# The middle tap and the bias of a width-3 depthwise convolution, moved from VectorE to ScalarE, in a two-layer diffusion backbone

## The chip, the cores and the metric

The kernel runs on one core of one Trainium2 chip. The metric is the device time of one execution in microseconds (us): the time before is the median of three runs, and a profile of one further execution shows where that time lies. The engines are named as the profile names them: PE is TensorE's matmul and PEld its weight load, DVE is VectorE, ACT is ScalarE, POOL is GpSimd, SP is SyncE, which here issues the loads.

## The reference, cut to what matters

Two layers (DEPTH 2) act on 128 context and 512 latent tokens of width 1024. Each layer has four attention branches, a merge, and a gated MLP with a centred depthwise convolution of width 3 between the up-projection and the activation:

```python
def _conv_ffn(h, lp):
    u = h @ lp['w_up']                      # D_FF = 2816, so 5632 channels
    up = jnp.pad(u, ((0, 0), (half, half), (0, 0)))
    acc = lp['conv_b'] + up[:, 0:T] * lp['conv_w'][0]
    for j in range(1, CONV_W):
        acc = acc + up[:, j:j + T] * lp['conv_w'][j]
    a, g = jnp.split(acc, 2, axis=-1)
    return (jax.nn.silu(g) * a) @ lp['w_down']
```

Context and latent tokens are convolved apart. Each residual branch is scaled by a gate that comes out of a linear map of SiLU(cond), the adaLN modulation: six sections of 1024 values a layer, two for each of shift, scale and gate. Section 5 is the MLP's gate.

## The kernel before

Activations lie with channels on the 128 partitions and the 640 tokens along the free axis, and each product is made in two halves of 320 columns. Every fp32 operand is split into a high part (written `wh`, `hH`: ScalarE) and a low part (`wl`, `hL`: VectorE, original minus high part), and a product is three matmuls: high by high, high by low, low by high (`passes`, L952).

The order of the instructions on each engine is made by a planner that runs when the program is built (L189 to L480). Pieces of work are generators. The dense ones (projections) are taken from one queue in a fixed order; the others (norms, attention, convolution, activation, modulation) run beside them by priority. The planner keeps an estimated clock for each engine: `act` (L292) adds 93 + 0.8333 ns for each element to ScalarE's clock, and 93 more for each scale or bias that is a tile; `clk("V", ...)` adds to VectorE's. Whatever may start by these clocks is written down next. The engines then run their instructions in the written order and wait at semaphores.

In the MLP, `up_gen` (L1373) makes one unit of 128 channels `u` in two halves of 24 matmuls each, and ScalarE moves the halves from PSUM to `u` (L386 to L390). `conv` (L1331) then makes `y` of 128x641 in three VectorE instructions: L1337 is the middle tap and the bias, and the two `stt` calls add the outer taps in place. `chain` (L1345) takes a pair of units, an `a` and a `g`: ScalarE's tanh, VectorE's products, a ScalarE and a VectorE split. `down_gen` (L1398) multiplies the result by `w_down`, group by group. Weights come in by SP into three buffers `raw`; ScalarE makes `wh`, VectorE `wl`.

The modulation for the later sections is worked off in the background by `ada_bg` (L752), in half sections: eight loads, each with two VectorE multiply-adds into two accumulators (L790 to L797), then for both accumulators a high part on ScalarE and a low part on VectorE (L804, L808), four matmuls by `selR` (L812), the split of the resulting row into `rowR`, high part on ScalarE, low part on VectorE (L815, L816), and after the second half the four matmuls `sel<-rowR` (L823). This generator does not go on while ScalarE's or VectorE's planned clock is more than 1000 ns ahead of PE's. `down_gen` begins only when section 5 is ready:

```python
        yield lambda: ("act", l, fs[0]) in done and ("ada", l, 3) in done
```

so the last dense work that may be written in front of the first down-projection of a layer is the seventh pair of up-projection units, and `sel<-rowR` of section 5 stands in front of the first down-projection in PE's order.

Of the kernel before, what the change touches and what calls it, by code (L numbers as in the profile page):

```python
# [13 lines left out]
AF = mybir.ActivationFunctionType  # L14
OP = mybir.AluOpType
# [173 lines left out]
def emit(nc, tc, t):  # L189
# [18 lines left out]
    class S:  # L208
        pe = 0.0
        cur = 0.0  # L210
        c = NC_SLOT
# [17 lines left out]
    def clk(e, cost, port=False):  # L229
        s = max(C[e], S.cur)  # L230
        if port:
            s = max(s, C["X"])
            C["X"] = s + cost - (130 if e == "G" else 0)
        C[e] = s + cost
        S.cur = s + cost + S.t[0]
# [15 lines left out]
    def Q(dt=F):  # L251
        return G(dt, False)

    def rel(*ts):
        for x in ts:
            k, _ = KIND.pop(id(x))
            if k == "c":
                S.c += 1
            else:
                S.g += 1  # L260
# [25 lines left out]
    def fsize(ap):  # L286
        n = 1
        for s in ap.shape[1:]:
            n *= s
        return n  # L290

    def act(out, in_, func, **kw):  # L292
        c = (52 if psum(in_) else 93) + 0.8333 * fsize(out)
        if TAB.get(func, tab[0]) != tab[0]:
            tab[0] = TAB[func]
            c += 1283
        for k in ("scale", "bias"):
            if not isinstance(kw.get(k, 0.0), (int, float)):
                c += 93
        if "accum_out" in kw:  # L300
            c += 93
        clk("A", c)
        nc.scalar.activation(out, in_, func, **kw)  # L303

    def psum(ap):
        return ap.tensor.space == bass.MemoryType.PSUM
# [38 lines left out]
    def stt(out, a, s, b, op0, op1):  # L345
        clk("V", (67 if isinstance(s, float) else 129) + 1.042 * fsize(out), two(a, b))
        nc.vector.scalar_tensor_tensor(out, a, s, b, op0=op0, op1=op1)  # L347
# [59 lines left out]
    def spawn(gen, prio, keep=(0, 0), lim=None):  # L407
        th = Th(gen, prio, keep, lim)
        th.ready = S.cur
        i = 0  # L410
        while i < len(ths) and ths[i].prio <= prio:
            i += 1
        ths.insert(i, th)
# [917 lines left out]
    def conv(l, f, s):  # L1331
        yield 1
        u = UB.pop((f, s))
        y = Q()
        c = VECS[l][:, V_CV:V_CV + 176].rearrange("p (c j) -> p c j", j=4)[:, s * NF + f]
        clk("V", 520)
        nc.vector.tensor_scalar(y[:, :641], u[:, 1:642], c[:, 1:2], c[:, 3:4], op0=OP.mult, op1=OP.add)  # L1337
        stt(y[:, :641], u[:, 0:641], c[:, 0:1], y[:, :641], OP.mult, OP.add)
        stt(y[:, :641], u[:, 2:643], c[:, 2:3], y[:, :641], OP.mult, OP.add)
        rel(u)  # L1340
        YB[f, s] = y
        if s == 1:
            spawn(chain(l, f), 2)

    def chain(l, f):  # L1345
        yield lambda: (f, 0) in YB
        yield 3
        a, g = YB.pop((f, 0)), YB.pop((f, 1))
        th = Q()
        H, L = Q(R), Q(R)  # L1350
        act(th[:, :641], g[:, :641], AF.Tanh, scale=0.5)
        yield
        stt(g[:, :641], th[:, :641], 1.0, g[:, :641], OP.add, OP.mult)
        tt(th[:, 0:128], a[:, 0:128], g[:, 0:128], OP.mult)
        tt(th[:, 128:640], a[:, 129:641], g[:, 129:641], OP.mult)
        rel(a, g)
        yield
        split_h(H[:, :NT], th[:, :NT], 0.5)
        yield
        split_l(H[:, :NT], L[:, :NT], th[:, :NT], 0.5)  # L1360
        rel(th)
        ACTS[f] = (H, L)
        yield
        done.add(("act", l, f))
# [8 lines left out]
    def up_gen(l, f, s, part):  # L1373
        yield N(c=1 if part != 1 else 0, cond=has("h4", l, 1, part if part < 2 else 1))
        gk = gate(l, 1, part if part < 2 else 1)
        u = u_tile(f, s) if part != 1 else UB[f, s]
        V = yield from W3("a", s, f, 8)
        for hh, (a, b) in enumerate(HC):
            if part < 2 and hh != part:
                continue  # L1380
            yield N(d=1)
            pd = PD()
            yield from half_mm(pd[:, :HN], V, 8, hH, hL, hh, gk=gk)
            S.cur = S.pe + S.t[1]
            if hh == 0:
                act(u[:, 1:129], pd[:, 0:128], AF.Copy)
                S.cur = S.pe + S.t[1]
                act(u[:, 130:322], pd[:, 128:320], AF.Copy)
            else:
                act(u[:, 322:642], pd[:, :HN], AF.Copy)  # L1390
            free("d")
        wrel()
        if part:
            spawn(conv(l, f, s), 2)
# [841 lines left out]
```

## Time and profile before

| | |
|---|---|
| median of three runs | 2325.96 us (2325.31 to 2327.69) |
| the profiled execution | 2329.46 us, of which the span from first to last instruction is 2327.7 us |
| mean granted TensorE clock | 0.991 of full speed |
| busy share of the span | PE 98%, DVE 77%, ACT 48%, POOL 13% |
| chain that ended last | PE 76%, DVE 13%, ACT 4%, DMA 3%, issue 3% |
| the MLP of layer 0, of layer 1 | about 730 to 1190 us, about 1870 to 2328 us |

Matmuls are pipelined, so PE's busy time is not its peak; the gaps between its instructions are what can be read. A wait is put down to the engine that released it last.

### The profile page before, as it was taken

To read this page: it belongs to the slowest core of one execution; us is meant where nothing else is said; L and a number is where in the kernel's file an instruction comes from. 1 tells how busy PE (TensorE), PEld (TensorE's weight loads), DVE (VectorE), ACT (ScalarE), POOL (GpSimd) and SP (SyncE) were. 2 spreads that over 40 slices of the span, in tenths; PEclk is the share of its full clock that TensorE was granted. 3 is DMA by queue.
4 is the path that set the end of the run, shared out by engine and by line. 5 is a ranking of instruction groups with operands and counts; after the bars stand their busy time and mean duration, and the time that the engine had idled before them with its cause. 6 is when DMAs were issued, how large, how long until landed. Compare 5 with 4: busy or idle time off the path is not lost.

```text
span 2327.7 us, 40730 instructions
## 1 busy us (share of the span) xinstructions
PE 2273.9 (98%) x15480; PEld 2195.2 (94%) x15480; DVE 1800.1 (77%) x3399; ACT 1125.4 (48%) x2419; POOL 300.1 (13%) x563
## 2 busy tenths in 40 slices
PE   8899999999999999999999999999999999999999
PEld 3899999999999999999999989999999999999999
DVE  5678878878779888766677788887879997565566
ACT  4467767664344323233355676666534542323232
POOL 0112112312021000000022121132111200000000
PEclk9999999999999999999999999999999999999999
DMA  7632323335554342322264332233456432221313
GB/s 255 235 122 73 112 82 110 100 127 175 196 186 137 105 155 93 125 78 68 87 202 155 121 114 82 87 111 109 145 179 225 172 114 85 85 74 59 98 51 132
DMA packets 114018, 292.18 MB, mean 126 GB/s; under 512 B 15840, under 2 KB 24736, under 8 KB 113824
## 3 DMA queue, kind: packets, MB, share of 16 engines
q1 hardware_dynamic: 105664, 258.43, 33.8%
q0 software_dynamic: 8160, 31.15, 3.6%
q8 instruction: 122, 2.00, 0.4%
q14 instruction: 72, 0.59, 0.1%
HBM read 257.59 MB, written 31.95 MB: 124 GB/s over the span
## 4 chain that ended last, share of the span: by engine, by line
PE 76%; DVE 13%; ACT 4%; DMA 3%; issue 3%; SPq 0%; POOL 0%; DVEq 0%; ACTq 0%; POOLq 0%
PE d L368 63%; PE ps L368 10%; DVE c L347 3%; PE po L368 2%; DVE wl L332 2%; DMA c<-w_ada 2%; DVE c L332 1%; ACT wh L303 1%; DVE p L347 1%; DVE hL L347 1%; DVE g L332 1%; ACT ps L303 1%; DMA g<-sp 1%; ACT c L325 1%; ACT c L303 0%
## 5 line engine op out<-in xcount | busy, mean ns | idle before, releaser
L368 PE MATMUL d<-hH,wh 128*128 128x320 f32 x2432 | 760.4, 313 | 0.4 <-ACT hH L303 0.4
L368 PE MATMUL d<-hL,wh 128*128 128x320 f32 x2432 | 754.7, 310 | 3.4 <-DVE hL L347 3.4
L368 PE MATMUL d<-hH,wl 128*128 128x320 f32 x2432 | 753.9, 310 | 0.8 <-DVE wl L332 0.8
L368 PEld LDWEIGHTS d<-hL,wh 128*128 128x128 f32 x2432 | 460.1, 189 | 7.6 <-DVE hL L347 5.0
L368 PEld LDWEIGHTS d<-hH,wh 128*128 128x128 f32 x2432 | 459.9, 189 | 4.1 <-ACT hH L303 0.7
L368 PEld LDWEIGHTS d<-hH,wl 128*128 128x128 f32 x2432 | 459.5, 189 | 1.1 <-DVE wl L332 1.1
L303 ACT ACTIVATE wh<-raw 128x1024 fp32r<-128x1024 f32 (+4 forms) x344 | 333.7, 971 | 206.2 <-PE d L368 178.4
L368 PE MATMUL d<-c,wh 128*128 128x320 f32 x1776 | 411.5, 311 | 2.8 <-DVE c L347 1.1
L332 DVE TENSOR_TENSOR wl<-raw,wh 128x1024 fp32r<-128x1024 f32 (+4 forms) x344 | 383.4, 1115 | 35.1 <-ACT wh L303 33.0
L303 ACT ACTIVATE c<-d 128x320 f32<-128x320 f32 (+2 forms) x376 | 130.7, 372 | 389.6 <-PE d L368 384.2
L368 PEld LDWEIGHTS d<-c,wh 128*128 128x128 f32 x1776 | 300.6, 189 | 7.8 <-DVE c L347 2.2
L368 PE MATMUL d<-c,wl 128*128 128x320 f32 x960 | 297.1, 309 | 0.0
L368 PE MATMUL d<-wh,hH 128*128 128x256 f32 (+1 forms) x720 | 208.7, 290 | 3.9 <-ACT wh L303 2.4
L347 DVE SCALAR_TENSOR_TENSOR c<-c,cs,c 128x512 f32<-128x512 f32 x266 | 198.0, 791 | 15.9 <-DMA c<-w_ada 15.9
L368 PE MATMUL d<-wh,hL 128*128 128x256 f32 (+1 forms) x720 | 205.1, 285 | 3.4 <-DVE hL L347 3.4
L368 PE MATMUL d<-wl,hH 128*128 128x256 f32 (+1 forms) x720 | 205.3, 285 | 1.0 <-DVE wl L332 1.0
L303 ACT ACTIVATE c<-c 128x641 f32<-128x641 f32 (+8 forms) x197 | 127.8, 665 | 161.1 <-DVE c L347 78.4
L368 PEld LDWEIGHTS d<-c,wl 128*128 128x128 f32 x960 | 180.9, 188 | 0.0
L347 DVE SCALAR_TENSOR_TENSOR c<-c,vec,c 128x641 f32<-128x641 f32 x174 | 154.6, 888 | 12.7 <-DVE c L347 0.5
L368 PE MATMUL d<-g,wh 128*128 128x320 f32 x656 | 158.9, 309 | 0.0
L1337 DVE TENSOR_SCALAR c<-c,vec 128x641 f32<-128x641 f32 x87 | 53.5, 614 | 124.7 <-ACT c L303 121.5
L368 PEld LDWEIGHTS d<-wh,hH 128*128 128x128 f32 x720 | 138.1, 192 | 5.1 <-ACT wh L303 2.6
(196 smaller groups left out, 3449.2 us busy)
## 6 DMA issues: line engine op xcount, KB each, us to landing
raw<-wst SPq DMA_DIRECT2D x264, 512.0 KB
c<-w_ada SPq DMA_DIRECT2D x184, 256.0 KB
mgd<-c POOLq DMA_DIRECT2D x46, 320.0 KB, 3.2
raw<-wst SPq DMA_DIRECT2D x32, 320.0 KB
c<-mgd SPq DMA_DIRECT2D x30, 320.0 KB
raw<-wst SPq DMA_DIRECT2D x32, 256.0 KB
c<-rpb SPq DMA_DIRECT2D x24, 320.0 KB
c<-xin SPq DMA_DIRECT2D x16, 320.0 KB
```

Of the source, the lines that this page charges most:

```text
L303: nc.scalar.activation(out, in_, func, **kw)
L325: nc.scalar.copy(out, in_)
L332: nc.vector.tensor_tensor(out, a, b, op=op)
L347: nc.vector.scalar_tensor_tensor(out, a, s, b, op0=op0, op1=op1)
L368: nc.tensor.matmul(out, lhsT, rhs, start=start, stop=stop, skip_group_check=True)
L1337: nc.vector.tensor_scalar(y[:, :641], u[:, 1:642], c[:, 1:2], c[:, 3:4], op0=OP.mult, op1=OP.add)
```

## The change

L1336 and L1337, a planned cost of 520 ns and one VectorE instruction, become one ScalarE activation with the function Identity, whose scale and bias are columns of the tile `vec`. The two VectorE instructions that follow read and write the same `y` as before. The convolution is made for 44 units in each of the two layers.

```diff
         c = VECS[l][:, V_CV:V_CV + 176].rearrange("p (c j) -> p c j", j=4)[:, s * NF + f]
-        clk("V", 520)
-        nc.vector.tensor_scalar(y[:, :641], u[:, 1:642], c[:, 1:2], c[:, 3:4], op0=OP.mult, op1=OP.add)
+        act(y[:, :641], u[:, 1:642], AF.Identity, scale=c[:, 1:2], bias=c[:, 3:4])
         stt(y[:, :641], u[:, 0:641], c[:, 0:1], y[:, :641], OP.mult, OP.add)
         stt(y[:, :641], u[:, 2:643], c[:, 2:3], y[:, :641], OP.mult, OP.add)
```

By `act` the planner now charges ScalarE 93 + 0.8333 x 641 + 2 x 93 = 813 ns, and since its clocks move, it writes some of the other work down in another place. On PE the dense matmuls keep their order. In both layers' MLPs the background matmuls of the modulation stand elsewhere among them; the attention parts of both layers are in the old order on every engine.

The first place is layer 0, section 5 of the modulation in front of the first down-projection. On PE before, `ps<-...selR` are the four matmuls of the second half section, `d1842` is the last half of an up-projection, `d1851` the first down-projection (its operands are `c` tiles):

```order
L368 MATMUL d1842_9830<-hH2_102,wl1819_9656 128x320
L368 MATMUL ps1843_9840<-c1829_9750,selR_89 2x512
L368 MATMUL ps1843_9840<-c1830_9751,selR_89 2x512
L368 MATMUL ps1843_9840<-c1831_9752,selR_89 2x512
L368 MATMUL ps1843_9840<-c1832_9753,selR_89 2x512
L368 MATMUL d1842_9830<-hH3_103,wh1815_9632 128x320
L368 MATMUL d1842_9830<-hL3_111,wh1815_9632 128x320
L368 MATMUL d1842_9830<-hH3_103,wl1819_9656 128x320
```

Fifteen matmuls of `d1842`, of which the last three rows are the first, follow the four, and then `sel<-rowR` and `d1851`. The same place on PE in the changed kernel, where the last half of the up-projection is `d1838` and the first down-projection `d1857`:

```order
L368 MATMUL d1838_9820<-hL7_115,wh1815_9623 128x320
L368 MATMUL d1838_9820<-hH7_107,wl1819_9646 128x320
L368 MATMUL ps1850_9873<-c1840_9850,selR_89 2x512
L368 MATMUL ps1850_9873<-c1841_9851,selR_89 2x512
L368 MATMUL ps1850_9873<-g1842_9852,selR_89 2x512
L368 MATMUL ps1850_9873<-g1843_9853,selR_89 2x512
L368 MATMUL ps1851_9882<-sel4_91,rowR_94 128x4 x4
L368 MATMUL d1857_9895<-c1739_9052,wh1822_9698 128x320
```

The four `selR` matmuls have moved behind the last up-projection, and nothing stands between them and `sel<-rowR`. VectorE at this place in the changed kernel, where `g1844` is the convolution of the unit that `d1838` completes, `c1841` and `g1843` are the low parts that `selR` reads, and `rowR` is the low part that `sel<-rowR` reads:

```order
L347 SCALAR_TENSOR_TENSOR g1794_9443<-g1796_9445,cs_124,g1794_9443 128x512
L347 SCALAR_TENSOR_TENSOR g1844_9856<-c1833_9779,vec0_128,g1844_9856 128x641 x2
L332 TENSOR_TENSOR wl1845_9860<-raw1820_9648,wh1839_9848 128x640
L332 TENSOR_TENSOR c1841_9851<-c1793_9442,c1840_9850 128x512
L332 TENSOR_TENSOR g1843_9853<-g1794_9443,g1842_9852 128x512
L347 SCALAR_TENSOR_TENSOR g1844_9856<-c1847_9866,g1844_9856 128x641
L332 TENSOR_TENSOR c1847_9866<-c1835_9791,g1844_9856 128x128
L332 TENSOR_TENSOR c1847_9866<-c1835_9791,g1844_9856 128x512
L332 TENSOR_TENSOR rowR_94<-ps1850_9873,rowR_94 2x512
```

The low parts for `selR` now stand behind the outer taps of the last unit; before they stood two units earlier, and the last unit's convolution came behind `rowR`. ScalarE at this place in the changed kernel; `c1833<-d1838` empties the last half of the up-projection, and `g1844<-c1833,vec0` is the new instruction:

```order
L303 ACTIVATE c1833_9779<-d1838_9820 128x320
L303 ACTIVATE wh1839_9848<-raw1820_9648 128x640
L303 ACTIVATE c1840_9850<-c1793_9442 128x512
L303 ACTIVATE g1842_9852<-g1794_9443 128x512
L303 ACTIVATE g1844_9856<-c1833_9779,vec0_128 128x641
L303 ACTIVATE c1847_9866<-g1844_9856 128x641
L303 ACTIVATE rowR_94<-ps1850_9873 2x512
```

The new instruction stands behind a weight split and the two high parts, all of them behind the emptying of `d1838`.

The second place is the same one in layer 1. VectorE before; `c4147` and `c4149` are the low parts for `selR`, `c4151` is the last unit's convolution:

```order
L347 SCALAR_TENSOR_TENSOR g4138_23156<-c4136_23154,g4137_23155 128x640
L332 TENSOR_TENSOR c4147_23241<-c4100_22862,c4146_23240 128x512
L332 TENSOR_TENSOR c4149_23243<-c4101_22863,c4148_23242 128x512
L1337 TENSOR_SCALAR c4151_23266<-c4140_23189,vec1_135 128x641
L347 SCALAR_TENSOR_TENSOR c4151_23266<-c4140_23189,vec1_135,c4151_23266 128x641 x2
L332 TENSOR_TENSOR wl4152_23270<-raw4127_23060,wh4150_23264 128x640
L332 TENSOR_TENSOR rowR_94<-ps4154_23274,rowR_94 2x512
```

And VectorE in layer 1 in the changed kernel, where `c4148` and `c4150` are those low parts:

```order
L347 SCALAR_TENSOR_TENSOR c4101_22869<-c4103_22871,cs_124,c4101_22869 128x512
L347 SCALAR_TENSOR_TENSOR c4151_23264<-c4140_23187,vec1_135,c4151_23264 128x641 x2
L332 TENSOR_TENSOR wl4152_23268<-raw4127_23056,wh4146_23256 128x640
L332 TENSOR_TENSOR c4148_23259<-c4100_22868,c4147_23258 128x512
L332 TENSOR_TENSOR c4150_23261<-c4101_22869,c4149_23260 128x512
L347 SCALAR_TENSOR_TENSOR c4151_23264<-c4154_23274,c4151_23264 128x641
L332 TENSOR_TENSOR c4154_23274<-c4142_23199,c4151_23264 128x128
L332 TENSOR_TENSOR c4154_23274<-c4142_23199,c4151_23264 128x512
L332 TENSOR_TENSOR rowR_94<-ps4157_23281,rowR_94 2x512
```

The low parts have moved from in front of the last unit's convolution to behind it, and `rowR` behind three more rows. PE in layer 1 has `selR`, `sel<-rowR` and the first down-projection directly behind the last up-projection in both kernels, and ScalarE stands there as in layer 0.

## Rows read from the trace of the kernel before

**Rows 1.** The page: busy us of each engine, share of the span, instructions.

```profile
PE 2273.9 (98%) x15480; PEld 2195.2 (94%) x15480; DVE 1800.1 (77%) x3399; ACT 1125.4 (48%) x2419; POOL 300.1 (13%) x563
```

**Rows 2.** Stretches: us, busy PE, PEld, DVE, ACT, POOL (instructions), granted clock, DMA.

```profile
730.00:1190.00 460.00, 459.38 (x3118) 455.64 (x3118) 355.76 (x549) 159.72 (x295) 21.79 (x128) 1.00 0.34 107
1870.00:2328.00 458.00, 450.08 (x3051) 448.39 (x3050) 302.27 (x450) 139.80 (x253) 6.39 (x117) 1.00 0.26 86
...
820.00:840.00 20.00, 20.00 (x138) 20.00 (x138) 19.90 (x37) 4.45 (x6) 0.00 (x0) 1.00 0.54 181
```

**Rows 3.** PE's waits in the two MLPs: us in total, times, longest.

```profile
PE d L368 <- ACT hH L303: 0.4, 1, 0.4
...
PE ps L368 <- DVE rowR L332: 3.7, 1, 3.7
```

**Rows 4.** PE in order of time, layer 1, around the first down-projection.

```profile
1950.73 1.08 PE L368 MATMUL ps<-c,selR 128*2 128x512 f32 x4
1955.50 0.61 PE L368 MATMUL ps<-sel,rowR 98*128 98x4 f32 x4 [3.68 <-DVE rowR L332]
1955.97 0.79 PE L368 MATMUL d<-c,wh 128*128 128x320 f32 x2
...
1959.49 0.31 PE L368 MATMUL d<-g,wh 128*128 128x320 f32 x1
```

**Rows 5.** The granted clock behind that wait: busy us of PE, PEclk.

```profile
1957.00:1959.00 2.00, 2.00 (x10) 0.50 0.06 20
```

**Rows 6.** ACT in order of time, layer 1, the same stretch.

```profile
1947.86 1.15 ACT L303 ACTIVATE c<-c 128x512 fp32r<-128x512 f32 x2
1950.93 0.44 ACT L303 ACTIVATE c<-d 128x320 f32<-128x320 f32 x1 [1.92 <-PE d L368]
1951.27 0.73 ACT L303 ACTIVATE wh<-raw 128x640 fp32r<-128x640 f32 x1
1952.02 0.58 ACT L303 ACTIVATE rowR<-ps 2x512 fp32r<-2x512 f32 x1
```

**Rows 7.** DVE in order of time, layer 1, the same stretch.

```profile
1949.58 1.29 DVE L332 TENSOR_TENSOR c<-c,c 128x512 fp32r<-128x512 f32 x2
1951.46 0.62 DVE L1337 TENSOR_SCALAR c<-c,vec 128x641 f32<-128x641 f32 x1 [0.60 <-issue]
1952.12 1.88 DVE L347 SCALAR_TENSOR_TENSOR c<-c,vec,c 128x641 f32<-128x641 f32 x2
1953.91 0.82 DVE L332 TENSOR_TENSOR wl<-raw,wh 128x640 fp32r<-128x640 f32 x1
1954.76 0.68 DVE L332 TENSOR_TENSOR rowR<-ps,rowR 2x512 fp32r<-2x512 f32 x1
1955.48 0.83 DVE L347 SCALAR_TENSOR_TENSOR c<-c,c 128x641 f32<-128x641 f32 x1
1956.34 0.89 DVE L332 TENSOR_TENSOR c<-c,c 128x128 f32<-128x128 f32 x2
```

**Rows 8.** PE in order of time, layer 0, around the first down-projection.

```profile
812.28 1.09 PE L368 MATMUL ps<-c,selR 128*2 128x512 f32 x4
813.21 0.31 PE L368 MATMUL d<-hH,wh 128*128 128x320 f32 x1
...
815.42 0.51 PE L368 MATMUL ps<-sel,rowR 98*128 98x4 f32 x4
815.78 0.54 PE L368 MATMUL d<-c,wh 128*128 128x320 f32 x2
```

**Rows 9.** Groups by line and shape: count, busy us, mean ns, idle before and releaser.

```profile
L1337 DVE TENSOR_SCALAR c<-c,vec 128x641 f32<-128x641 f32 x87 | 53.5, 614 | 124.7 <-ACT c L303 121.5 <-issue 2.9
L303 ACT ACTIVATE c<-c 128x641 f32<-128x641 f32 x42 | 31.2, 743 | 67.6 <-DVE c L347 65.5 <-issue 2.1
L303 ACT ACTIVATE hH<-c,ad,gs 128x320 fp32r<-128x320 f32 x8 | 4.9, 643 | 0.0
L303 ACT ACTIVATE hH<-c,ad,gs 128x128 fp32r<-128x128 f32 x8 | 3.9, 482 | 10.6 <-DVE gs L631 10.6
```

## The prediction, made before the changed kernel ran

> **What bounds the kernel now.** I read the page's first part, then the busy time by stretches, then PE's waits in the two MLPs, since the convolution runs nowhere else, and last PE, ACT and DVE in order of time where PE waits. The page has PE busy for 98% of the span and DVE for 77% [rows 1]. PE is pipelined, so that figure alone proves little; what counts is that in layer 0's MLP PE is busy 459.38 of 460 us and that its longest wait there is 0.4 us [rows 2, 3]. DVE is busy 355.76 us of the same 460 and ACT 159.72 [rows 2]; in places DVE is full, as with 19.90 of 20 us between 820 and 840, and PE still runs through [rows 2]. So DVE is loaded but hidden: the MLP lasts as long as its matmuls do. Layer 1's MLP is the same but for one wait of 3.7 us, PE for DVE's `rowR` [rows 3]. There PE ends the four `selR` matmuls, has nothing but `sel<-rowR` written next, and stands until 1955.50 [rows 4]. Between 1957 and 1959 the clock is granted at 0.50, that is 1.2 of 2.4 GHz [rows 5]. The matmuls' usual pitch is 0.147 us (15 of them between 813.21 and 815.42 in [rows 8]); from 1955.97 to 1959.49 thirteen take 3.52 us where they would take 1.91, so the wait costs another 1.6 us in clock [rows 4].
>
> **What the change removes.** 88 DVE instructions of 614 ns, 54 us of DVE [rows 9]. PE waited for DVE for almost nothing, so as busy time this is worth nothing; it could gain only what is in the 3.7 + 1.6 us of layer 1.
>
> **What it adds.** 88 activations on ACT. None of this shape with two tile operands is in the trace. The lower bound is 743 ns, the tanh of 128x641 without them [rows 9]. With both, 128x128 takes 482 ns and 128x320 643 ns, 0.84 ns for each further column, which gives 912 ns at 641 [rows 9]. I take 0.91 us, since that row has the same operands: 80 us on ACT. ACT has 300 of 460 us free in layer 0's MLP [rows 2], so this too is hidden as busy time. Two rules of the notes frame it. The Trainium skill, ScalarE: Activation LUTs, section Rules for kernel authors, says to give multiplications and additions to VectorE and not to ScalarE; by that rule each moved instruction is 0.3 us dearer here, 26 us in all if ScalarE set the pace, which the rows on its free time speak against. The Trainium skill, Perfetto Trace Analysis, section Optimizing Scalar/DVE Operations, says that moving work to ScalarE may pay where VectorE is saturated; by that rule the late `rowR` of layer 1 would come earlier, and the trace agrees with its premise only between such points as 820 to 840.
>
> **What it moves.** This is the term that decides. ACT has its weight split in front of the new instruction, so DVE's outer taps wait for PSUM emptying, weight split and tap, where the old tap waited for the emptying alone. The planner sees its DVE clock run ahead more often, which holds back the background modulation. Hence the end of section 5 is written later: in both layers the low parts that `selR` reads now stand on DVE behind the last unit's outer taps, which need the new activation, which needs the emptying of the very last up-projection half. Behind that half PE has nothing written but `selR`, `sel<-rowR` and the down-projections. So PE waits for a whole chain over ACT and DVE, twice. I add it up from T, where PE would start `selR` (1950.73 in layer 1):
>
> - ACT starts emptying 0.20 after T, and its weight split at 0.54 [rows 6]. The next instruction can start 0.75 later, at 1.3 [rows 6].
> - The two high parts take 1.15 together [rows 6]: they end at 2.35, as instructions in a row overlap by about 0.1.
> - The new activation, 0.91, ends at 3.2.
> - DVE's two outer taps, 1.88, end at 5.1; the weight's low part, 0.82, at 5.8; the two low parts, 1.29, at 7.05 [rows 7].
> - The last `selR` matmul needs some 0.4 at the low clock (two such matmuls take about half of the 1.08 of four at full clock [rows 4]): 7.45.
> - ACT's `rowR`, 0.58, ends at 8.1 [rows 6]. DVE meanwhile runs the rows in front of its own `rowR`, 0.83 and 0.89, and ends them at 8.6 [rows 7].
> - DVE's `rowR`, 0.68, ends at 9.3 [rows 7]; `sel<-rowR` starts 0.06 later and the first down-projection 0.47 after that [rows 4]: T + 9.8.
>
> I counted the rows in front back from T with the same durations, and DVE comes to the outer taps some 2.5 us before the activation is done, so a backlog of that size changes nothing.
>
> In layer 0 before, T is 812.28 and the down-projection starts at 815.78, 3.50 later, of which 15 up-projection matmuls are 2.21 [rows 8]: the place cost 1.3. Now it costs 9.8, so 8.5 more. PE then stands as in layer 1, and I add the same 1.6 of clock: **10.1 us**. In layer 1 the place took 1955.97 - 1950.73 = 5.2 [rows 4], now 9.8: **4.6 us**, with the clock's loss paid already. The sum is **14.7 us**. The other `selR` sets of the MLPs have moved too, but each keeps at least 20 matmuls, 3 us, between the last half it depends on and itself, and the attention parts are unchanged, so I put both at nothing; if DVE is late there, each costs a microsecond or two.
>
> Bounds: with the activation at 743 ns each place is 0.2 shorter. The clock may cost layer 0 nothing, or, as PE stands longer, twice 1.6 in both places: 14.7 - 0.4 - 1.6 = 12.7 to 14.7 + 1.6 + 1.6 = 17.9. The profiled execution took 2329.46 us, 1.8 more than its span and 3.5 more than the median of 2325.96. On its own time the sum is 2344.2; on the median, which I predict, **2340.7 us**, 2338.7 to 2343.9 by these bounds.
>
> **The rivals.**
>
> - *Faster: DVE's relief ends the wait.* Layer 1's `rowR` stood behind an old tap of 0.62 [rows 7], and with 54 us less on DVE the modulation could be done before the last up-projection half; the whole 3.7 + 1.6 would go, 2320.7 us. It decides where the low parts come before T. Against it speaks the written order, which puts them behind an instruction that reads that half. 5%.
> - *No change.* The chain is hidden or made good later: the planned stall would be paid back by a wait elsewhere that shrinks. But apart from these places PE's waits in the MLPs are under 1 us [rows 3], so there is nothing to be paid back from. 2322 to 2330 us. 5%.
> - *Slower by less: only part of the chain is new.* PE's and ACT's queues overlap more than I count, or the clock stays up: two thirds of the sum, about 10 us, 2336; 2331 to 2337. 12%.
> - *Slower by more: ACT becomes late throughout.* The tap and the tanh that waits for DVE (65.5 us of ACT's idle time in 42 waits [rows 9]) stand in front of the emptying of PSUM; with three PSUM tiles of 24 matmuls each, 3.5 us, PE feels it only if ACT is late by two halves, 7 us. If the excess of 0.3 us for each of 88 instructions then came through, it would add 26 us: 2367. The same result as the rule for VectorE above. 6%.
>
> **How the numbers follow.** The forecast has 72%, and 2337 to 2345 as its own range. To leave no more than 2 in 10 outside I take in most of the smaller sum and a few new waits of a microsecond at the moved sets: 2333 to 2347. A difference under 0.2%, 4.7 us, is about what a measurement of this kernel can't tell from no change. Faster by more than that: 4%, most of the first rival; within it: 8%, the rest of it, the second rival and the weak end of the third; slower: 88%.
>
> **What the changed profile would show.** If I am right: the new activation near 0.91 us; PE's waits for ACT and DVE in front of `selR` and `sel<-rowR` in both MLPs, some 8 us together at each place (most of it in front of `selR`, about 2 in front of `sel<-rowR`), with PEclk at 0.5 behind them; DVE less busy by about 54 us and ACT more by about 80; the attention parts as long as they were. A step fails if the time from the last up-projection matmul to the first down-projection isn't near 9.8 us, if layer 0 shows no gap, or if new waits for PSUM appear among the up-projections.

## The result and the profile after

The changed kernel is slower. It was measured three times, each time beside the kernel before on the same chip:

| | median after, us | median before, us | difference, us | ratio, 95% interval |
|---|---|---|---|---|
| first | 2347.97 (4 runs) | 2325.72 (4) | +22.3 | 1.0088 [1.0071, 1.0106] |
| second (e5) | 2345.75 (5) | 2329.97 (27) | +15.8 | 1.0075 [1.0061, 1.0089] |
| third (e11) | 2348.66 (5) | 2328.74 (15) | +19.9 | 1.0079 [1.0065, 1.0093] |

The forecast was 2340.7, which is 14.7 above the median of before, with a range from 2333 to 2347; the median of the first measurement lies 1 us above the range. Taken by their ratios on the median of before, 2325.96, the three are 2346.4, 2343.4 and 2344.3. On the chips of the later measurements the kernel before is 3 to 4 us slower and its own runs lie further apart (2324.59 to 2334.57 in the third), so experiments are compared with the kernel before of their own chip.

The page of the changed kernel (2348.34 us, span 2346.5), the line that answers to [rows 1]: busy us of each engine, share of the span, instructions.

```profile
PE 2278.0 (97%) x15480; PEld 2200.2 (94%) x15480; DVE 1747.2 (74%) x3311; ACT 1198.4 (51%) x2507; POOL 298.4 (13%) x563
```

VectorE lost 53 us of work and ScalarE took 73, less than the 80 of 88 activations: in the rows below the new instruction begins 0.1 us before the one in front of it ends; PE's share fell from 98% to 97%. The groups by line and shape (count, busy us, mean ns of one, idle time of the engine before them, and what ended it) show the new instruction and the outer taps behind it:

```profile
L303 ACT ACTIVATE c<-c,vec 128x641 f32<-128x641 f32 x86 | 78.6, 914 | 0.0
L347 DVE SCALAR_TENSOR_TENSOR c<-c,vec,c 128x641 f32<-128x641 f32 x172 | 152.8, 888 | 217.3 <-ACT c L303 208.0 <-DVE c L347 0.5
```

The activation takes 914 ns; 86 of the 88 stand in this row, the other two write a tile of another name. VectorE now stands 208.0 us in front of the outer taps, waiting for ScalarE; before, it stood 121.5 in front of the middle tap [rows 9]. Nearly all of that is idle time beside a busy PE. Where it is not, PE's waits show it. These are all of PE's waits in layer 0's MLP between 735 and 1198 us (us in total, times, longest), where [rows 3] had 0.4:

```profile
PE ps L368 <- DVE c L332: 4.2, 1, 4.2
PE ps L368 <- ACT c L303: 1.7, 1, 1.7
PE ps L368 <- DVE rowR L332: 1.5, 1, 1.5
```

Layer 1's MLP has the same three waits with the same numbers, in place of the one of 3.7 in [rows 3]. Here they are in PE's order of time, layer 0 (start, us, engine, line, instruction, count, and in brackets the idle time before it):

```profile
813.06 0.31 PE L368 MATMUL d<-hH,wl 128*128 128x320 f32 x1
815.04 0.39 PE L368 MATMUL ps<-c,selR 128*2 128x512 f32 x1 [1.67 <-ACT c L303]
819.62 0.59 PE L368 MATMUL ps<-c,selR 128*2 128x512 f32 x1 [4.19 <-DVE c L332]
820.00 1.06 PE L368 MATMUL ps<-g,selR 128*2 128x512 f32 x2
822.61 1.01 PE L368 MATMUL ps<-sel,rowR 98*128 98x4 f32 x4 [1.54 <-DVE rowR L332]
823.48 0.88 PE L368 MATMUL d<-c,wh 128*128 128x320 f32 x2
...
830.56 0.46 PE L368 MATMUL d<-c,wh 128*128 128x320 f32 x2
```

The last up-projection matmul starts at 813.06, so T is 813.21; the first down-projection starts at 823.48, T + 10.27. In [rows 8] it came 3.50 after T, 2.21 of it work. The same place of layer 1:

```profile
1964.20 0.31 PE L368 MATMUL d<-hH,wl 128*128 128x320 f32 x1
...
1974.62 0.88 PE L368 MATMUL d<-c,wh 128*128 128x320 f32 x2
```

What PE waits for is in the orders of ACT and then of DVE in layer 1, where T is 1964.35; they answer to [rows 6, 7]:

```profile
1964.55 0.44 ACT L303 ACTIVATE c<-d 128x320 f32<-128x320 f32 x1 [3.02 <-PE d L368]
1964.88 0.73 ACT L303 ACTIVATE wh<-raw 128x640 fp32r<-128x640 f32 x1
1965.51 1.14 ACT L303 ACTIVATE c<-c 128x512 fp32r<-128x512 f32 x2
1966.55 0.91 ACT L303 ACTIVATE c<-c,vec 128x641 f32<-128x641 f32 x1
...
1972.24 0.58 ACT L303 ACTIVATE rowR<-ps 2x512 fp32r<-2x512 f32 x1 [2.04 <-PE ps L368]
```

```profile
1967.49 1.88 DVE L347 SCALAR_TENSOR_TENSOR c<-c,vec,c 128x641 f32<-128x641 f32 x2 [2.77 <-ACT c L303]
1969.28 0.82 DVE L332 TENSOR_TENSOR wl<-raw,wh 128x640 fp32r<-128x640 f32 x1
1970.02 1.29 DVE L332 TENSOR_TENSOR c<-c,c 128x512 fp32r<-128x512 f32 x2
1971.22 0.82 DVE L347 SCALAR_TENSOR_TENSOR c<-c,c 128x641 f32<-128x641 f32 x1
1972.08 0.89 DVE L332 TENSOR_TENSOR c<-c,c 128x128 f32<-128x128 f32 x2
1973.01 0.68 DVE L332 TENSOR_TENSOR rowR<-ps,rowR 2x512 fp32r<-2x512 f32 x1
```

ScalarE empties PSUM, makes the weight's high part, then the two high parts of the modulation, and only then the tap. VectorE stands 2.77 us for it and then works without a gap through the outer taps, the weight's low part and the low parts that `selR` needs. The first down-projection starts at 1974.62, again T + 10.27.

### The profile page after: what moved, and what is told of

Same layout as the page of the kernel before. It is cut to its first block, busy times and chain, and to the rows that moved or that the text cites. A ratio compares the mean times of both kernels' runs of the same rounds, so it can differ in the third digit from the quotient of the medians.

```text
span 2346.5 us, 40719 instructions
## 1 busy us (share of the span) xinstructions
PE 2278.0 (97%) x15480; PEld 2200.2 (94%) x15480; DVE 1747.2 (74%) x3311; ACT 1198.4 (51%) x2507; POOL 298.4 (13%) x563
## 4 chain that ended last, share of the span: by engine, by line
PE 77%; DVE 12%; ACT 4%; DMA 4%; issue 3%; SPq 1%; POOL 0%; DVEq 0%; ACTq 0%; POOLq 0%
PE d L368 65%; PE ps L368 9%; PE po L368 2%; DVE wl L332 2%; DVE c L347 2%; DVE c L332 1%; DMA c<-w_ada 1%; DMA raw<-wst 1%; ACT wh L303 1%; DMA g<-sp 1%; DVE g L332 1%; ACT ps L303 1%; DVE p L347 1%; DVE hL L347 1%; ACT c L303 1%
## 5 line engine op out<-in xcount | busy, mean ns | idle before, releaser
L368 PE MATMUL d<-c,wh 128*128 128x320 f32 x1824 | 422.5, 312 | 3.1 <-DVE c L347 1.4
L368 PEld LDWEIGHTS d<-c,wh 128*128 128x128 f32 x1824 | 309.3, 189 | 8.2 <-DVE c L347 2.5
L347 DVE SCALAR_TENSOR_TENSOR c<-c,vec,c 128x641 f32<-128x641 f32 x172 | 152.8, 888 | 217.3 <-ACT c L303 208.0
L368 PE MATMUL d<-c,wl 128*128 128x320 f32 x976 | 302.7, 310 | 0.0
L347 DVE SCALAR_TENSOR_TENSOR c<-c,cs,c 128x512 f32<-128x512 f32 x252 | 188.4, 795 | 17.2 <-DMA c<-w_ada 17.0
L368 PE MATMUL d<-g,wh 128*128 128x320 f32 x608 | 147.0, 310 | 0.0
L303 ACT ACTIVATE ps<-ps,sl 128x320 f32<-128x320 f32 (+3 forms) x224 | 113.8, 509 | 57.5 <-DVE sl L1815 37.4
L368 PEld LDWEIGHTS d<-wh,hL 128*128 128x128 f32 x720 | 138.8, 193 | 4.4 <-DVE hL L347 3.8
```

Source lines behind the costliest of these rows:

```text
L368: nc.tensor.matmul(out, lhsT, rhs, start=start, stop=stop, skip_group_check=True)
```

## The experiments

**e1: the tap on ScalarE in the order of before.** The planner still charges VectorE, so only the instruction changes its engine; PE's 15480 matmuls stand in the traces in the order of the kernel before.

```diff
         clk("V", 520)
-        nc.vector.tensor_scalar(y[:, :641], u[:, 1:642], c[:, 1:2], c[:, 3:4], op0=OP.mult, op1=OP.add)
+        nc.scalar.activation(y[:, :641], u[:, 1:642], AF.Identity, scale=c[:, 1:2], bias=c[:, 3:4])
```

> The middle tap and the bias run on ScalarE, but the planner still charges VectorE 520 ns for them, so the order on every engine is that of the kernel before. Theory A (the moved order makes the stalls, the tap's engine does not): no stall in layer 0; in layer 1 the last outer taps, and rowR behind them, come 0.8 later than before, so the wait of 3.7 becomes about 4.5. In all 0.5 to 2 us above the kernel before: 2326 to 2328. Rival B (the activation's own cost on ScalarE, 0.91 for 0.61 and in line in front of the emptying of PSUM): nearly all of the 22 us stays, 2342 or more. Rival C (the relief of VectorE is worth something once the order is kept): under 2322.

Measured: 2332.24 against 2329.75, ratio 1.0009 [1.0000, 1.0019]. Layer 0's place has no wait; PE's waits in layer 1's MLP from 1890 on are one row:

```profile
PE ps L368 <- DVE rowR L332: 4.4, 1, 4.4
```

That is 0.7 more than the 3.7 of [rows 3]; 0.8 was expected. The whole is +2.5, a little over the 0.5 to 2 expected, with an interval from 0 to 4.4. 88 activations of 0.91 us on ScalarE are hidden, and rival B falls: by the interval at most 4.4 us can be the tap's engine.

**e2: the new order with the tap on VectorE.**

```diff
-        clk("V", 520)
+        clk("A", 93 + 0.8333 * 641 + 2 * 93)
         nc.vector.tensor_scalar(y[:, :641], u[:, 1:642], c[:, 1:2], c[:, 3:4], op0=OP.mult, op1=OP.add)
```

> The order of the changed kernel on every engine, with the tap written as the old VectorE instruction (the planner charges it to ScalarE as the changed kernel does). Theory A: both stalls stay, each shorter by the part of the chain that ScalarE's weight split and tap made: VectorE can begin its outer taps at about T + 1.3 and not at T + 3.1, so the last up-projection to the first down-projection takes 8 to 9 and not 10.3; in all 2342 to 2346. Rival B (the tap's engine is the cost): 2322 to 2330. Rival C (part of the excess comes from transfers and clock outside the two places, with the moved order): those parts stay as in the changed kernel, too.

PE's matmuls stand in the order of the changed kernel. Measured: 2338.95 against 2329.75, +9.2, ratio 1.0044 [1.0029, 1.0059]. Layer 0's place in PE's order:

```profile
815.30 0.39 PE L368 MATMUL ps<-c,selR 128*2 128x512 f32 x1 [1.67 <-ACT c L303]
818.13 0.58 PE L368 MATMUL ps<-c,selR 128*2 128x512 f32 x1 [2.44 <-DVE c L332]
...
821.11 1.02 PE L368 MATMUL ps<-sel,rowR 98*128 98x4 f32 x4 [1.55 <-DVE rowR L332]
821.99 0.88 PE L368 MATMUL d<-c,wh 128*128 128x320 f32 x2
```

The middle wait is 2.44 for 4.19, and the rest stands: T is 813.47 (815.30 less the same 1.83 as above), so the down-projection starts at T + 8.5, as expected. The total is a miss: 2342 to 2346 was expected, counted from the first measurement's 2348. Against the +15.8 and +19.9 of the other two, the +9.2 is 6.6 to 10.7 less, and the two shorter waits are 3.5 of it. Counted by rows as for the changed kernel below, the two gates of e2 (T + 8.5 at both, the 36 matmuls behind them in 6.67 and 6.79 us) cost 11.7 us, inside the interval of 6.8 to 13.7, where the changed kernel's cost 15.5. So the new order alone, which only the planner's charge has made, costs about half of the loss by the times, and three quarters by the rows, with not one instruction moved to ScalarE.

**e3: the gate moved.** The changed kernel; the first down-projection halves may run before section 5 is ready, and only their residual additions wait.

```diff
-        yield lambda: ("act", l, fs[0]) in done and ("ada", l, 3) in done
+        yield lambda: ("act", l, fs[0]) in done
+        pend = []
...
-                    S.cur = S.pe + S.t[1]
-                    resid(l, 5, m, x[m], pd, hh)
-                    free("d")
+                    pend.append((m, pd, hh))
+                    if len(pend) < 3 and ("ada", l, 3) not in done:
+                        continue
+                    yield has("ada", l, 3)
+                    for pm, pp_, ph in pend:
+                        S.cur = S.pe + S.t[1]
+                        resid(l, 5, pm, x[pm], pp_, ph)
+                        free("d")
+                    pend = []
```

> The changed kernel, but the first three down-projection halves no longer wait for section 5; only their residual additions do. 45 matmuls, 6.6 us, then stand in front of selR, where the chain up to selR took 6.4 to 6.8. Theory A: the waits in front of selR (4.2 and 1.7 at each place) go, and what is left at each place is the wait for rowR in front of sel<-rowR, 1.5 by itself and up to 2.6, since nothing stands between, and about 1.2 of clock: 6 to 8 us at the two places together, where the changed kernel has 20 and the kernel before 7. In all 2327 to 2335. Rival B (ScalarE's tap is the cost) or rival C (transfers and clock elsewhere): 2340 or more.

Measured: 2334.60 against 2329.75, +4.9, ratio 1.0022 [1.0012, 1.0031]. PE's waits in layer 0's MLP up to 1190 us; layer 1's are the same two rows:

```profile
PE ps L368 <- DVE rowR L332: 2.4, 1, 2.4
PE d L368 <- DVE c L347: 1.3, 1, 1.3
```

The waits in front of `selR` are gone, and `rowR` has its 2.4. The 1.3 was not expected: three halves fill all three PSUM tiles, and the fourth waits for the residual that empties one. With ScalarE's tap unchanged, most of the loss is gone, so it sat at the gate.

**e4 and e6: the modulation held back less, with the tap on either engine.** `ADA_LIM` is the limit of 1000 ns on the planned clocks; e4 is the changed kernel, e6 the kernel before.

```diff
-ADA_LIM = 1000.0
+ADA_LIM = 1500
```

> The changed kernel with the background modulation held back only when VectorE's or ScalarE's planned clock is 1500 ns ahead of PE's, not 1000. selR of section 5 then stands 115 matmuls in front of the first down-projection in both layers, and the gate is open when it comes. Theory A: no wait above 1 us at the two places, so layer 1's old 3.7 + 1.6 goes as well: 2320 to 2326, a microsecond or two more if other selR sets now wait. Rival B: 2340 or more. Rival C (transfers and clock outside the places cost 3 to 5): 2324 to 2330 with the attention part of layer 1 as long as in the changed kernel.

> The kernel before with the background modulation held back at 1500 ns, not 1000: the partner of the changed kernel with that limit, which differs from it in the tap's engine alone (and in what the planner makes of that). Theory A (the tap's engine is worth nothing where no chain of it stands in front of PE): the two within 2 us of each other; layer 1's wait of 3.7 is gone. Rival B (the activation costs by itself): this one faster by 5 or more. Rival D (VectorE's 54 us are worth something without the stall): this one slower by 2 or more.

Measured: e4 2329.04 against 2329.75, ratio 0.9998 [0.9989, 1.0008]; e6 2329.76 against 2329.97, ratio 0.9997 [0.9988, 1.0005]. Both lose the waits at the gate in both layers, the 3.7 of before with them, and the two engines for the tap come out alike. Neither gains the 5 us that layer 1's wait was worth. For e4 they were expected, 2320 to 2326 in all; its ratio on the median of before gives 2325.5, at the upper end. They went into new waits elsewhere: summed over all rows, PE's waits from 1700 to 1870 us, ahead of layer 1's MLP, are 4.7 in the kernel before and 10.2 in e4, 9.6 in e6. The longest groups there in e6; the first and the last are new, the second was 1.1 and the third 2.1:

```profile
PE d L368 <- DVE g L347: 2.2, 2, 1.2
PE d L368 <- DVE c L347: 2.0, 3, 1.1
PE d L368 <- DVE hL L347: 1.6, 4, 1.0
PE ps L368 <- DVE c L332: 1.0, 1, 1.0
```

**e7 and e9: the gate moved in the order of before, with the tap on either engine.** e7 is the kernel before with e3's edit of the gate, e9 the same with e1's edit of the tap.

> The kernel before with the gate moved: up to three down-projection halves no longer wait for section 5. In layer 0 the order is that of the kernel before; in layer 1 21 matmuls, 3.1 us, stand in front of selR and 24 more in front of sel<-rowR. Theory A: layer 1's wait of 3.7 and the clock behind it, 1.6, go: 4 to 5.5 us under the kernel before. If only the wait goes and the clock falls elsewhere: 2 to 4 under.

> The kernel before with the gate moved (four microseconds under the kernel before), and the tap on ScalarE in that same order. No chain over ScalarE stands in front of PE any more: in layer 1 rowR would be ready some 5.6 after the last up-projection and sel<-rowR stands 6.6 after it. Theory A: no wait at either place, and the same time as with the tap on VectorE, within 2 us: 2 to 6 under the kernel before. Rival B (the activation costs by itself): 5 or more above the kernel before. Rival D (VectorE's 54 us are worth something): 7 or more under.

Measured: e7 2325.91 against 2329.97, -4.1, ratio 0.9985 [0.9976, 0.9994]; e9 2323.72 against 2328.74, -5.0, ratio 0.9980 [0.9970, 0.9991]. PE's waits in layer 1's MLP from 1890 on are one row in each of them, the residual's (here e9's), and layer 0's place has none:

```profile
PE d L368 <- DVE c L347: 1.1, 1, 1.1
```

Both are faster than either kernel of this case. The wait of 3.7 and the clock behind it were worth 4 to 5 us, near the 5.3 that the prediction had given them (the intervals reach from 1.4 to 5.6 and from 2.1 to 7.0). With no chain in front of PE the tap on ScalarE costs nothing that shows, nor does it gain: PE's matmuls stand in the same order in both, the intervals of e7 and e9 overlap, and a difference of some 3 us would be hidden in them. The two ran on different chips, each beside the kernel before.

**e5, e8 and e11: the same programs again.** e5 and e11 are the changed kernel, e8 the kernel before, unedited.

> The changed kernel again, beside the experiments. Theory A: its waits at the two places are the same 4.2, 1.7 and 1.5 as in its first profile, and it lies above the kernel with the tap on VectorE in the new order by twice 1.8 and up to 2 of clock: 13 to 15 us above the kernel before of the same chip. Theory C (clock and transfers outside the two places are fixed parts of the change): 22 us above, and the 2.4 that the attention part of layer 1 took longer is there again. If that part is as long as in the kernel before this time, it was of the run and not of the change.

> The kernel before again, for a second profile of the same program: the waits of PE must be the same (rowR 3.7 in layer 1, hL 2.1), and the stretches at the low clock show how much of the time lost there is of the run: the same within 0.5 us if it belongs to the program, 3 us or more apart if it does not.

> The changed kernel a third time, beside the two above: the waits at the two places the same (4.2, 1.7, 1.5), 14 to 18 us above the kernel before if the second measurement is the typical one, 22 if the first was.

The times of e5 and e11 stand in the table: e5 lies 0.8 us over the 13 to 15 expected, e11 between its two cases. e8 took 2330.02 against 2329.97. The waits at the gates are the same to 0.1 us in every profile of a program. Other things are not. Between two norms, one behind layer 0's MLP and one ahead of layer 1's, lies the whole attention of layer 1; both are marked by an instruction of POOL. These are POOL's rows for the changed kernel, then for e5, the same program, and then for e1, which has the order of before:

```profile
1207.08 1.82 POOL L877 TENSOR_TENSOR s<-s,mhalf 128x3 f32<-128x3 f32 x1 [6.71 <-DVE s L873]
1834.33 0.87 POOL L877 TENSOR_TENSOR s<-s,mhalf 128x3 f32<-128x3 f32 x1 [9.73 <-DVE s L873]
```

```profile
1208.15 2.13 POOL L877 TENSOR_TENSOR s<-s,mhalf 128x3 f32<-128x3 f32 x1 [6.71 <-DVE s L873]
1833.05 0.88 POOL L877 TENSOR_TENSOR s<-s,mhalf 128x3 f32<-128x3 f32 x1 [9.73 <-DVE s L873]
```

```profile
1197.97 2.13 POOL L877 TENSOR_TENSOR s<-s,mhalf 128x3 f32<-128x3 f32 x1 [6.71 <-DVE s L873]
1825.22 0.88 POOL L877 TENSOR_TENSOR s<-s,mhalf 128x3 f32<-128x3 f32 x1 [9.72 <-DVE s L873]
```

The stretch takes 627.25 in the first profile of the changed kernel, 624.90 in its second, 626.30 in its third (e11) and 627.25 in e1; in the two profiles of the kernel before it takes 624.68 and 623.74. The 2.6 us by which the changed kernel's first profile is longer there than the first of the kernel before are no fixed part of the change, since e5 has 0.2 of them, and theory C falls for them. They show as waits: PE stands there in the first profile 2.1 us for ScalarE's `ps` and 1.2 for its `p`, in e5 0.5 and 0.3.

**e10: PE kept busy through the wait.** The changed kernel, with spare matmuls that nothing reads.

```diff
+    def spare(pt, n):
+        r = ACTS[0][0]
+        for _ in range(n):
+            nc.tensor.matmul(pt[:, :320], r[:, :128], r[:, :320], start=True, stop=True, skip_group_check=True)
...
+            if s == 5 and hf == 1:
+                spare(pt, 38)
             for i, x in enumerate(hl):
...
+            if s == 5:
+                spare(pt, 12)
             for m in range(4):
```

> The changed kernel with its order and its chains as they are, but PE has spare matmuls of 128x320, 38 in front of selR of section 5 and 12 in front of its sel<-rowR, in both layers; their results are overwritten and used by nothing. The first down-projection can start no earlier than the chain lets it, about 9.5 to 10.3 after the last up-projection. Theory A: the clock stays at 1.0 through both places, so that the extra time of the matmuls behind them, 1.7 to 2.4 in each layer, goes, and the four selR run at full clock: 3 to 5 us under the changed kernel. If the clock's fall is not from PE's standing: the same time as the changed kernel, or slower by what the spare work overshoots.

Measured: 2338.57, +9.8 on the kernel before, ratio 1.0043 [1.0031, 1.0056], where e11 on the same chip is +19.9, 1.0079. That is 10 us under the changed kernel, where 3 to 5 was expected. PE in order of time in layer 0, for e10 and then for e11:

```profile
811.21 0.31 PE L368 MATMUL d<-hH,wl 128*128 128x320 f32 x1
811.35 5.74 PE L755 MATMUL ps<-c 128*128 128x320 f32 x38
...
817.78 0.40 PE L368 MATMUL ps<-c,selR 128*2 128x512 f32 x1 [0.45 <-DVE c L332]
...
820.76 0.61 PE L368 MATMUL ps<-sel,rowR 98*128 98x4 f32 x4 [0.23 <-DVE rowR L332]
821.23 0.54 PE L368 MATMUL d<-c,wh 128*128 128x320 f32 x2
...
826.59 0.46 PE L368 MATMUL d<-c,wh 128*128 128x320 f32 x2
```

```profile
813.49 0.31 PE L368 MATMUL d<-hH,wl 128*128 128x320 f32 x1
...
823.90 0.88 PE L368 MATMUL d<-c,wh 128*128 128x320 f32 x2
...
831.77 0.46 PE L368 MATMUL d<-c,wh 128*128 128x320 f32 x2
```

The stretch from 820 to 826 us in both, e10 first (us, busy PE, PEld, DVE, ACT, POOL with their instructions, granted clock, DMA):

```profile
820.00:826.00 6.00, 5.76 (x41) 5.50 (x40) 3.88 (x9) 0.98 (x2) 0.00 (x0) 1.00 0.29 95
```

```profile
820.00:826.00 6.00, 4.41 (x15) 3.14 (x16) 3.91 (x7) 1.32 (x2) 0.00 (x0) 0.50 0.57 188
```

With PE busy the clock stays at 1.00, 2.4 GHz; with PE standing it is granted at 0.50. The chain itself is almost as long: the spare matmuls start at T = 811.35 and the down-projection at T + 9.88, the 9.8 of the prediction, 0.39 less than with the clock down. The first 36 down-projection matmuls take 5.36 us here (821.23 to 826.59), 7.87 in e11 (823.90 to 831.77). So the clock's fall, and its price of 0.4 + 2.5 at this place, comes from PE's standing. In layer 1 the price is 0.4 + 2.1 (36 matmuls in 5.35 us for 7.46). That makes 5.4 us at the two places. The spans of the two profiled executions are 7.6 apart (2340.2 and 2347.8), and some 2.3 of them are there before the first spare matmul: the last up-projection matmul starts at 811.21 in e10 and at 813.49 in e11. So the spare matmuls themselves are worth the 5.4 that the rows show, which the ratios, 8 us apart, give or take 4, don't contradict.

## Why the prediction was right, and where it was short

- **VectorE's 54 us are worth nothing: right.** With the stall out of the way, the two engines for the tap give the same time twice, to within the 3 us that the intervals leave: e4 and e6 (0.9998 and 0.9997 of the kernel before) and e7 and e9 (0.9985 and 0.9980).
- **ScalarE's 80 us are hidden: right.** Forecast 0.91 us each, measured 0.914. The price of 0.3 us for each moved tap is in the rows (0.914 for 0.614 [rows 9]), and e1 shows that it does not reach the end: at most 0.19% by the interval, 4.4 us, where it would be 26. The Trainium skill, ScalarE: Activation LUTs, section Rules for kernel authors, would keep multiplications and additions on VectorE; for the single instruction these rows agree. The Trainium skill, Perfetto Trace Analysis, section Optimizing Scalar/DVE Operations, lets work move to ScalarE where VectorE is saturated; no run here shows a gain from it.
- **The order decides: right.** Both places appeared where the prediction put them, in front of `selR` and of `sel<-rowR`. e4 and e9 remove them in two ways with the tap left on ScalarE, e3 removes those in front of `selR`, and e2 keeps them all with the tap on VectorE. The other `selR` sets that moved cost nothing, as forecast: between 735 and 1198 us and from 1890 us on, the three rows above are all of PE's waits.
- **The chain: right step by step.** In layer 1 the outer taps start at T + 3.14 (forecast 3.2), the low parts end at T + 6.96 (7.05), DVE's `rowR` ends at T + 9.34 (9.3). The waits came out as 1.7 + 4.2 + 1.5, some 7.4 for the 8 that were forecast; with `selR` and `sel<-rowR` themselves the first down-projection is at T + 10.27, where 9.8 was forecast. The last 0.4 was counted at full clock and ran at half, as e10 shows by its 9.88.
- **The clock: the term that was too small.** The prediction took 1.6 us in layer 0 and nothing more in layer 1. The first 36 matmuls behind the gate take 5.36 us at full clock. In layer 0 they took 7.08, 7.80 and 7.87 in the three profiles of the changed kernel, a loss of 1.7 to 2.5. In layer 1 they took 6.69, 7.80 and 7.46, and 6.89 and 8.02 in the two of the kernel before, so there the loss had been paid already, as forecast. The single row from which the 1.6 came [rows 4] lies near the low end of what such a wait costs, 1.3 to 2.7. The prediction had one such wait to read from; its bounds, 12.7 to 17.9, leave room for the rest.

The sum by rows for the first profile: layer 0 10.27 - 1.29 + 1.7 = 10.7, layer 1 10.27 - 5.24 - 0.2 = 4.8, together 15.5 for the 14.7 forecast. The two later profiles of the changed kernel, set against e8, give 15.8 (e5: 11.4 + 4.4) and 15.5 (e11: 11.5 + 4.1). For e5 and e8, which ran on one chip, that is all there is: the spans are 15.7 apart (2343.6 and 2327.9). In the first profile the spans are 18.8 apart, so 3.3 lie outside the gates, of which 2.6 are the attention part that e5 does not have; in e11, against e8 of another chip, 4.3 lie outside. The ratios of 1.0075 to 1.0088 are 17 to 21 us on 2326, 1 to 5 more than the gates. So the gates are the part of the loss that every profile shows, and the prediction's sum for them was short by about 1 us; what lies outside them goes from nothing to 4 us with the execution. Whether the changed kernel meets such longer stretches more often than the kernel before, three profiles of the one and two of the other don't settle; it stays open.

Of the rivals, *faster* and *no change* fell with the result. *Slower by less* fell too: the chain came out at its full length. *Slower by more*, ScalarE late throughout, is excluded by e1 and e9; the time came out above the forecast for other reasons: the clock behind layer 0's gate, and what lies outside the gates.

## What to carry to other kernels

Where a planner or a scheduler places the work by estimated costs, moving one instruction to another engine is two edits, and they can be measured apart: keep the old charge with the new engine (e1), and the new charge with the old engine (e2). Before counting what a relieved engine gains, look for the one point where the in-order engine that sets the time has nothing else written, and add up the whole chain behind it; work that can be written between the chain and its reader (e7, e9: 4 to 5 us) is worth more than 54 us off an engine that nobody waits for. A wait taken out of one place is a gain only if the order does not put a new one elsewhere, as the larger limit did.

## What the runs showed of the hardware that was not expected

- The same wait in the same program costs a different time in clock from one execution to the next: behind layer 0's gate 36 matmuls took 7.08, 7.80 and 7.87 us, behind layer 1's in the kernel before 6.89 and 8.02. In some executions the clock falls at a place where it stays up in others. Here is the stretch from 1864 to 1874 us in the two profiles of the kernel before, the granted clock standing behind POOL's column:

```profile
1864.00:1874.00 10.00, 8.48 (x44) 7.97 (x44) 9.79 (x15) 3.81 (x6) 0.00 (x0) 0.83 0.45 157
```

```profile
1864.00:1874.00 10.00, 8.24 (x52) 7.71 (x53) 9.83 (x16) 3.91 (x7) 0.00 (x0) 1.00 0.48 157
```

- The two profiles of the kernel before differ by more than the 0.5 us that would have made the clock a fixed part of the program and by less than the 3 that would have made it the run's alone: e8 loses 1.1 us more behind layer 1's gate and, by the rows above, 1.7 us (0.17 of 10) less at the norm.
- Spare matmuls that nobody reads made the changed kernel faster, 2338.57 for 2348.66 on the same chip, with the order of all its other instructions as it was; by the rows, 5.4 of these 10 us are theirs.
